# Hybrid decoder block on one core: the sums of the second MLP weight, on VectorE or by adding transfers

## The chip, the core and the metric

The kernel runs on one core of a Trainium2 chip. The core has five engines, each with a queue of its own that is worked off in order: PE (TensorE, matrix products), DVE (VectorE), ACT (ScalarE), POOL (GpSimd) and SP (SyncE, which here only issues transfers). SP, ACT and POOL can all issue transfers; these run on the same sixteen DMA engines. Queues wait for each other by semaphores.

The metric is the time of one execution in microseconds (us), the median of several runs.

## What is computed

One layer of a decoder: a mixer of two parts (gated linear attention and an S5 state-space layer), its output projection, and an MLP with a squared ReLU, over 512 tokens (and 16 meta tokens) of width 1024, in float32. The change lies in the MLP:

```python
hn = rmsnorm(h, g_ffn_pre[l])
f = jnp.square(jax.nn.relu(hn @ w_ff1[l])) @ w_ff2[l]
h = h + rmsnorm(f, g_ffn_post[l])
```

`w_ff1` is 1024 x 4096 and `w_ff2` 4096 x 1024. Below, f stands for the squared ReLU, kept in SBUF with its 4096 features on the partitions (32 blocks of 128) and the 512 tokens beside.

## The kernel before

**Products in three passes.** Each float32 operand is split into a rounded part ("hi", made by ScalarE, L152) and the rest ("lo", made by VectorE: L165 for weights of the first product, L1305 for those of the second). TensorE then makes three matmuls, hi x hi, hi x lo and lo x hi. A weight tile of 512 KB comes in on SyncE's queue as `wraw` (three buffers), is split into `whi` and `wlo` (three buffers each), and feeds the matmuls.

**The first MLP product.** For each of the 32 blocks of features (m), a tile of w1 is loaded (L158) and split, and 24 matmuls give the block; `relu2` (L1265) puts ReLU on ScalarE and the square on VectorE into f. The first three blocks run early, before all of hn is there. hh and hl are the two parts of hn, transposed.

**The second MLP product, by seven products.** f and w2 are taken as 2 x 2 blocks: tokens in two halves of 256, feature blocks even and odd, output columns in two halves of 512. `quarters` gives a11, a12 (first half of the tokens, even and odd blocks) and a21, a22 (second half); `b_of(k, n)` gives the blocks of w2, b11 to b22. Seven products of such blocks, with sums of blocks as operands, take the place of eight. Sums of f: s1 = a21 + a22, s2 = s1 - a11, s3 = a11 - a21, s4 = a12 - s2, made by VectorE in SBUF. Sums of w2: T1 = b12 - b11, T2 = b22 - T1, T3 = b22 - b12, T4 = b21 - T2.

**The sums of w2.** `weight_sums(j)` (L1254) does this for one pair of blocks j of 16: POOL loads 1 MB of w2 (`w2raw`, L1257), VectorE makes four sums of 128 x 512 (`w2t`, L1259 to L1262), POOL writes them, 1 MB, to DRAM (`t2d`, L1263). It is called after every second block of the first product, and twice behind it. There are two buffers of each kind.

**How the seven products run.** `product` (L1330) takes eight tiles; for each it calls `operands`, which loads 512 KB of w2 or of a sum from DRAM (L1302) and splits both sides, and then `step` twice, 12 matmuls in all. The order of the seven is a11 b11, s1 T1, s2 T2, a12 b21, s3 T3, s4 b22, a22 T4. X, Y and Z are the pairs of PSUM banks in which they are gathered. At the start of the products ScalarE's queue issues five loads of 512 KB (L1290, L1294): the gain `gff` and h of the four token tiles, which are wanted only at the end, when the second RMSNorm and the residual are done.

**What sets the order.** The code is written per tile; a scheduler puts it into the queues, and brings work forward where its operands and buffers allow. TensorE is held to the written order where `pinned` is set, which is so in the seven products and not from the first product's fourth block to its end. SBUF that one pool gives back is used by the next: the tiles of the pool `pout` (gff, h, c and others, from L1288) lie where hh, hl and the buffers of the sums were, so writing them waits until those are read.

## Time and profile before

| | |
|---|---|
| median of 3 runs | 907.79 us (906.01 to 909.96) |
| the profiled execution, its own time | 905.13 us |
| its span, first to last instruction | 903.4 us |
| mean granted TensorE clock | 0.997 |
| first MLP product from its fourth block | 583.0 to 743.1 us |
| the seven products | 743.1 to about 893 us |
| the end behind them (norm, residual, stores) | to 903.4 us |

A row of a group reads: line, engine, operation, output<-input by the program's names, shapes, how many; then busy time in us and the mean of one in ns; then the time that the engine stood idle just before them, and what ended it. A row of waits reads: who waited <- for whom: us in total, how often, the longest. A row of stretches gives the length, for each engine its busy time and how many instructions, the granted clock, the mean busy share of the sixteen DMA engines, and GB/s. A DMA row gives the issuing queue, how many, KB each, and the median us from issue to landing. Times in a timeline are us from the span's start.

A matmul of 512 columns reads 0.39 us, but matmuls overlap; what counts is the distance of their starts.

### The profile page before, as it was taken

The page shows a single profiled execution, that of the slowest core. Times are in us where ns is not written, and L with a number is a line of the kernel's source. Part 1 is how long each engine was busy: PE and PEld are TensorE (multiplying, and loading weights), DVE is VectorE, ACT ScalarE, POOL GpSimd, SP SyncE. Part 2 cuts the span into 40 slices and gives each one's busy share as a digit, 9 for nine tenths or more (in the row PEclk, how much of TensorE's full clock was granted, in tenths as well). Part 3 has the DMA queues.
Part 4 walks back from the last instruction along what each step waited for, and adds up shares of the span by engine and source line. Part 5 has one row for each costly group of instructions (what it writes and reads, how often), then busy time and mean ns, then how long its engine had stood idle before and what let it go on. Part 6 is the DMA issues. An engine that isn't in the chain of part 4 may idle for free.

```text
span 903.4 us, 13494 instructions
## 1 busy us (share of the span) xinstructions
PE 889.7 (98%) x4994; PEld 759.5 (84%) x4994; DVE 669.9 (74%) x1204; ACT 407.5 (45%) x667; POOL 88.4 (10%) x166
## 2 busy tenths in 40 slices
PE   8999999999999999999999999999999999999996
PEld 6899899898988888888888888988877888888885
DVE  7779998887877699876344765767866448778786
ACT  6362355466563444225222544422322326665763
POOL 1311100010101201103000000111220000000001
PEclk9999999999999999999999999999999999999998
DMA  7824644444435546468645772599999337656564
GB/s 211 218 96 131 192 113 111 104 120 112 105 110 134 161 106 178 125 188 267 184 144 147 214 209 70 188 364 369 391 397 320 112 105 269 209 188 201 171 210 139
DMA packets 171955, 166.68 MB, mean 185 GB/s; under 512 B 22397, under 2 KB 137153, under 8 KB 171890
## 3 DMA queue, kind: packets, MB, share of 16 engines
q1 hardware_dynamic: 155920, 110.48, 43.1%
q0 software_dynamic: 14768, 51.34, 15.1%
q10 hardware_dynamic: 1202, 4.00, 1.4%
q8 instruction: 39, 0.64, 0.3%
q14 instruction: 26, 0.21, 0.1%
HBM read 131.42 MB, written 34.37 MB: 184 GB/s over the span
## 4 chain that ended last, share of the span: by engine, by line
PE 83%; DMA 8%; DVE 4%; issue 3%; ACT 1%; POOL 1%; DVEq 0%; POOLq 0%
PE mm L60 58%; PE sm L60 22%; DMA w2raw<-in_w_ff_dram 8%; PE sm L65 3%; DVE wlo L165 1%; DVE w2t L1262 0%; DVE w2t L1260 0%; DVE w2t L1259 0%; POOL t2d L1263 0%; DVE xn L314 0%; DVE w2t L1261 0%; DVE xl L195 0%; DVE c L1368 0%; PE mm L65 0%; DVE f L1268 0%
## 5 line engine op out<-in xcount | busy, mean ns | idle before, releaser
L152 ACT ACTIVATE whi<-wraw 128x1024 fp32r<-128x1024 f32 x160 | 168.5, 1055 | 234.9 <-PE mm L60 182.7
L60 PE MATMUL mm<-xh,whi 128*128 128x512 f32 (+2 forms) x544 | 182.8, 336 | 0.3 <-ACT xh L152 0.3
L60 PE MATMUL mm<-xh,wlo 128*128 128x512 f32 (+2 forms) x544 | 178.9, 329 | 0.2 <-DVE wlo L165 0.2
L60 PE MATMUL mm<-xl,whi 128*128 128x512 f32 (+2 forms) x544 | 178.6, 328 | 0.3 <-DVE xl L195 0.3
L165 DVE TENSOR_TENSOR wlo<-wraw,whi 128x1024 fp32r<-128x1024 f32 x104 | 126.9, 1221 | 55.0 <-ACT whi L152 50.1
L60 PEld LDWEIGHTS mm<-xh,whi 128*128 128x128 f32 x544 | 102.8, 189 | 10.9 <-issue 1.2
L60 PEld LDWEIGHTS mm<-xh,wlo 128*128 128x128 f32 x544 | 102.7, 189 | 9.5 <-DVE wlo L165 0.4
L60 PEld LDWEIGHTS mm<-xl,whi 128*128 128x128 f32 x544 | 102.9, 189 | 8.9 <-DVE xl L195 0.5
L60 PE MATMUL mm<-hh,wlo 128*128 128x512 f32 (+1 forms) x280 | 104.1, 372 | 1.7 <-DVE wlo L165 1.7
L60 PE MATMUL mm<-hh,whi 128*128 128x512 f32 (+1 forms) x280 | 104.0, 371 | 0.0
L60 PE MATMUL mm<-hl,whi 128*128 128x512 f32 (+1 forms) x280 | 103.8, 371 | 0.0
L1305 DVE TENSOR_TENSOR wlo<-wraw,whi 128x1024 fp32r<-128x1024 f32 x56 | 68.4, 1223 | 23.4 <-ACT whi L152 23.4
L60 PE MATMUL sm<-wlo,fh 128*128 128x512 f32 x192 | 74.8, 390 | 0.0
L60 PE MATMUL sm<-whi,fl 128*128 128x512 f32 x192 | 74.7, 389 | 0.0
L60 PE MATMUL sm<-whi,fh 128*128 128x512 f32 x192 | 74.7, 389 | 0.0
L60 PEld LDWEIGHTS mm<-hh,wlo 128*128 128x128 f32 x280 | 52.7, 188 | 11.6 <-DVE wlo L165 2.5
L60 PEld LDWEIGHTS mm<-hh,whi 128*128 128x128 f32 x280 | 52.7, 188 | 9.1
L60 PEld LDWEIGHTS mm<-hl,whi 128*128 128x128 f32 x280 | 52.7, 188 | 8.9
L152 ACT ACTIVATE fh<-f 128x512 fp32r<-128x512 f32 x48 | 30.2, 630 | 49.9 <-PE sm L60 27.1
L60 PE MATMUL mm<-gh,whi 128*128 128x512 f32 x128 | 49.8, 389 | 0.0
L60 PE MATMUL mm<-gl,whi 128*128 128x512 f32 x128 | 49.8, 389 | 0.0
L60 PE MATMUL mm<-gh,wlo 128*128 128x512 f32 x128 | 49.8, 389 | 0.0
(413 smaller groups left out, 1575.5 us busy)
## 6 DMA issues: line engine op xcount, KB each, us to landing
wraw<-in_w_ff_dram SPq DMA_DIRECT2D x56, 512.0 KB, 4.8
wraw<-in_w_in_dram SPq DMA_DIRECT2D x48, 512.0 KB, 4.3
w2raw<-in_w_ff_dram POOLq DMA_DIRECT2D x16, 1024.0 KB, 9.3
t2d<-w2t POOLq DMA_DIRECT2D x16, 1024.0 KB, 7.1
wraw<-t2d SPq DMA_DIRECT2D x32, 512.0 KB, 3.8
wraw<-in_w_glu_dram SPq DMA_DIRECT2D x16, 512.0 KB, 3.9
M<-kpad SPq DMA_DIRECT2D x64, 64.0 KB, 2.5
wraw<-in_w_o_gla_dram SPq DMA_DIRECT2D x8, 512.0 KB, 4.5
```

The costliest lines, as they stand in the source:

```text
L60: ins = nc.tensor.matmul(*args, **kw)
L65: ins = nc.tensor.transpose(*args, **kw)
L152: S.activation(dst, src, AF.Copy, scale=scale)
L165: V.tensor_sub(lo, raw, f32(hi))
L1305: V.tensor_sub(bl, raw, f32(bh))
```

## The change

The signs of the seven products are turned so that every sum of w2 is made by additions alone: s1 = a21 - a22, s2 = s1 - a11, s3 = a11 - a21, s4 = a12 + s2, and T1 = b11 + b12, T2 = T1 + b22, T3 = b12 + b22, T4 = T2 + b21. Where a result has the wrong sign, it is subtracted at the end instead of added. The sums of w2 are no longer made by VectorE but by transfers that add to what stands at their destination in SBUF (`accum_op=ALU.add`), all issued by POOL.

T2 and T4 are made in eight chains of six transfers of 512 KB: load b11, add b12, add b22, write T2 to DRAM, add b21, write T4 to DRAM. Four chains run interleaved (buffers `acc`), then four more. Two transfers are issued behind each block of the first product from the fourth on: ScalarE copies one element of the block's ReLU into `flags`, POOL copies it into `seen`, and the transfers stand behind that copy on POOL's queue.

T1 and T3 are made as they are used: `fetch_sum` loads b11 or b22 on SyncE's queue into a buffer `added` (five of them), POOL adds b12 to it, and `operands` splits that buffer. It is called four tiles ahead of use; for the first four tiles this is in the last four tiles of the product before. DRAM holds two sums instead of four.

```diff
-    td2 = mk(dr, [4, NJ, P, 512], tag="t2d")
+    td2 = mk(dr, [2, NJ, P, 512], tag="t2d")
...
-        V.tensor_add(s1[:, 2 * jj : 2 * jj + 2], a21, a22)
+        V.tensor_sub(s1[:, 2 * jj : 2 * jj + 2], a21, a22)
         V.tensor_sub(a21, a11, a21)
...
-    def weight_sums(j):
-
-        raw = mk(pw2, [P, 2, D], tag="w2raw", bufs=2)
-        nc.gpsimd.dma_start(raw, w2[2 * j * P : (2 * j + 2) * P, :].rearrange("(k p) n -> p k n", p=P))
-        t_ = mk(pw2, [P, 4, 512], tag="w2t", bufs=2)
-        V.tensor_sub(t_[:, 0], raw[:, 0, 512:], raw[:, 0, :512])
-        V.tensor_sub(t_[:, 1], raw[:, 1, 512:], t_[:, 0])
-        V.tensor_sub(t_[:, 2], raw[:, 1, 512:], raw[:, 0, 512:])
-        V.tensor_sub(t_[:, 3], raw[:, 1, :512], t_[:, 1])
-        nc.gpsimd.dma_start(td2[:, j].rearrange("i p n -> p i n"), t_)
+    def weight_sums(jj):
+
+        acc = mk(pw2, [P, 2, 512], tag="acc", bufs=4)
+        nc.gpsimd.dma_start(acc, b_of(0, 0)(jj))
+        yield
+        nc.gpsimd.dma_start(acc, b_of(0, 1)(jj), accum_op=ALU.add)
+        yield
+        nc.gpsimd.dma_start(acc, b_of(1, 1)(jj), accum_op=ALU.add)
+        yield
+        nc.gpsimd.dma_start(t_of(0)(jj), acc)
+        yield
+        nc.gpsimd.dma_start(acc, b_of(1, 0)(jj), accum_op=ALU.add)
+        yield
+        nc.gpsimd.dma_start(t_of(1)(jj), acc)
+        yield
...
     def relu2(m, ps):
         r_ = mk(pff, [P, SEQ], tag="relu", bufs=2)
         S.activation(r_, ps, AF.Relu)
         V.tensor_mul(f[:, m], r_, r_)
+        S.copy(flags[:, m : m + 1], r_[:1, :1])
+        return G.tensor_copy(seen[:, m : m + 1], flags[:, m : m + 1])
...
+    todo = [interleaved([weight_sums(g + i) for i in range(4)]) for g in range(0, NJ // 2, 4)]
+    todo = (step for chain in todo for step in chain)
     for m in range(EARLY, MF):
         ps = bank("mm")
         feat_tile(load_w(w1[:, m * P : (m + 1) * P])[0], hh, hl, 0, SEQ, ps)
-        relu2(m, ps)
+        there = relu2(m, ps)
         if m % 4 == 3:
             early_sums(m // 4)
-        if m % 2 == 0:
-            weight_sums(m // 2 - 2)
-    for j in (NJ - 2, NJ - 1):
-        weight_sums(j)
+
+        with tc.issue_after(there.ins):
+            for _ in range(2):
+                next(todo, None)
...
+    def fetch_sum(b, jj):
+
+        raw = added[b, jj] = mk(po_, [P, 2, 512], tag="added", bufs=5)
+        nc.sync.dma_start(raw, b_of(0, 0)(jj) if b == "T1" else b_of(1, 1)(jj))
+        nc.gpsimd.dma_start(raw, b_of(0, 1)(jj), accum_op=ALU.add)
+
     def operands(a, b, jj):
-        raw = mk(wp, [P, 2, 512], tag="wraw", bufs=3)
-        nc.sync.dma_start(raw, b)
+        if (b, jj) in added:
+            raw = added.pop((b, jj))
+        else:
+            raw = mk(wp, [P, 2, 512], tag="wraw", bufs=3)
+            nc.sync.dma_start(raw, b(jj))
...
+    LEAD_SUMS = 4
...
+            if following and jj >= n - LEAD_SUMS:
+                fetch_sum(following, jj - n + LEAD_SUMS)
+            if isinstance(b, str) and jj + LEAD_SUMS < n:
+                fetch_sum(b, jj + LEAD_SUMS)
...
-        V.tensor_sub(a12, a12, a11)
+        V.tensor_add(a12, a12, a11)
...
-    product(X, a_of(0), b_of(0, 0), True)
+    product(X, a_of(0), b_of(0, 0), True, following="T1")
     take([c[:, left] for c in cs_[:2]], X)
-    product(Y, s1_of, t_of(1), True, to_s2)
+    product(Y, s1_of, "T1", True, to_s2)
     take(p5, Y)
-    product(X, a_of(0), t_of(2), False)
+    product(X, a_of(0), t_of(0), False)
     take([c[:, right] for c in cs_[:2]], X)
-    product(Z, a_of(1), b_of(1, 0), True, closes=True)
+    product(Z, a_of(1), b_of(1, 0), True, closes=True, following="T3")
...
-    product(X, a_of(2), t_of(3), False, to_s4)
+    product(X, a_of(2), "T3", False, to_s4)
     take([c[:, right] for c in cs_[2:]], X)
     for t in range(2):
-        V.tensor_add(cs_[2 + t][:, right], cs_[2 + t][:, right], p5[t])
+        V.tensor_sub(cs_[2 + t][:, right], p5[t], cs_[2 + t][:, right])
...
-        V.tensor_add(cs_[t][:, right], cs_[t][:, right], Y[t])
+        V.tensor_sub(cs_[t][:, right], Y[t], cs_[t][:, right])
```

How the queues stand, at three places. First SyncE's queue at the start of the seven products, with the semaphores that each row waits for (DVE: a buffer was split; PE: matmuls have read; DMAHW and DMASW: transfers have landed). Before, from the first product's fifth tile (`wraw_7397`, counted as tile 4 from 0) to the second product's first two tiles, which are T1 from DRAM:

```order
L1302 DMA wraw_7397<-in_w_ff_dram 128x2x512 [waits DMAHW2_49,DVE_49]
L1302 DMA wraw_7419<-in_w_ff_dram 128x2x512 [waits DMAHW3_49,DVE_49]
L1302 DMA wraw_7441<-in_w_ff_dram 128x2x512 [waits DMAHW4_49,DVE_49]
L1302 DMA wraw_7463<-in_w_ff_dram 128x2x512 [waits DMAHW5_49,DVE_49]
L1302 DMA wraw_7487<-t2d_6063 128x2x512 [waits DMAHW6_49,DMASW4_49,DMAHW7_49,DMASW2_49,DVE_49]
L1302 DMA wraw_7510<-t2d_6063 128x2x512 [waits DMASW6_49,DMAHW4_49,DMASW0_49,DVE_49]
```

After, from the same fifth tile (now `wraw_7394`) to the third product's first tile (`wraw_7675`, T2 from DRAM); `wraw_7419`, `wraw_7444` and `wraw_7469` are tiles 5, 6 and 7 of the first product:

```order
L1344 DMA wraw_7394<-in_w_ff_dram 128x2x512 [waits DMAHW2_49,DVE_49]
L1336 DMA added_7391<-in_w_ff_dram 128x2x512 [waits DMASW5_49,DMASW4_49,DMASW6_49,DMASW0_49,PE_49]
L1336 DMA added_7416<-in_w_ff_dram 128x2x512
L1344 DMA wraw_7419<-in_w_ff_dram 128x2x512 [waits DMAHW3_49,DVE_49]
L1336 DMA added_7441<-in_w_ff_dram 128x2x512 [waits DMAHW4_49]
L1336 DMA added_7466<-in_w_ff_dram 128x2x512 [waits DMAHW6_49]
L1336 DMA added_7493<-in_w_ff_dram 128x2x512 [waits DMAHW0_49,DMASW7_49]
L1344 DMA wraw_7444<-in_w_ff_dram 128x2x512 [waits DMAHW1_49,DVE_49]
L1344 DMA wraw_7469<-in_w_ff_dram 128x2x512 [waits DMAHW5_49,DMAHW2_49,DVE_49]
L1344 DMA wraw_7675<-t2d_6063 128x2x512 [waits DMAHW3_49,DMASW4_49,DVE_49]
```

Two loads of T1 stand before the first product's tile 5 and three more before tile 6; the first of them waits for TensorE to have made the first MLP product's last matmul.

Second VectorE's queue in the first MLP product. Before:

```order
L1259 TENSOR_TENSOR w2t_6758<-w2raw_6756 128x512
L1261 TENSOR_TENSOR w2t_6758<-w2raw_6756 128x512
L1260 TENSOR_TENSOR w2t_6758<-w2raw_6756,w2t_6758 128x512
L1262 TENSOR_TENSOR w2t_6758<-w2raw_6756,w2t_6758 128x512
L165 TENSOR_TENSOR wlo_6538<-wraw_6535,whi_6537 128x1024
L1268 TENSOR_TENSOR f_6061<-relu_6445 128x512
```

After:

```order
L165 TENSOR_TENSOR wlo_6512<-wraw_6509,whi_6511 128x1024
L1294 TENSOR_TENSOR f_6061<-relu_6423 128x512
L165 TENSOR_TENSOR wlo_6550<-wraw_6547,whi_6549 128x1024
L1294 TENSOR_TENSOR f_6061<-relu_6461 128x512
L1350 TENSOR_TENSOR fl_7354<-f_6061,fh_7353 128x512
```

The four sums that stood ahead of a split and waited for w2raw are gone.

Third POOL's queue at the end of the chains. Before, it goes from load to write and back, up to the last block:

```order
L1257 DMA w2raw_7218<-in_w_ff_dram 128x2x1024
L1263 DMA t2d_6063<-w2t_7144 128x4x512
L1257 DMA w2raw_7262<-in_w_ff_dram 128x2x1024
L1263 DMA t2d_6063<-w2t_7220 128x4x512
L1257 DMA w2raw_7270<-in_w_ff_dram 128x2x1024
```

After, with the waits:

```order
L1277 DMA t2d_6063<-acc_6660 128x2x512 [waits DMASW0_49]
L1277 DMA t2d_6063<-acc_6662 128x2x512 [waits DMASW1_49]
L1296 COPY seen_6068<-flags_6067 1x1 [waits Activation_49]
L1277 DMA t2d_6063<-acc_6700 128x2x512 [waits DMASW2_49]
L1277 DMA t2d_6063<-acc_6702 128x2x512 [waits DMASW3_49]
L1296 COPY seen_6068<-flags_6067 1x1 [waits Activation_49] x5
L1337 DMA added_7391<-in_w_ff_dram 128x2x512 [waits DMAHW6_49,DVE_49,PE_49]
```

The chains' last transfers stand five blocks before the end of the first MLP product (the five copies behind them), and the adding transfers of T1 come next, each behind its load.

28 lines of the change are left out of this document (20 added, 8 removed).

## The prediction

> **What bounds the kernel now.** I read the page first, then the stretches of the second half, then who waits for whom there, then the DMA's landing times at the start of the seven products. The page:
>
> ```profile
> span 903.4 us, 13494 instructions
> ...
> PE 889.7 (98%) x4994; PEld 759.5 (84%) x4994; DVE 669.9 (74%) x1204; ACT 407.5 (45%) x667; POOL 88.4 (10%) x166
> ...
> w2raw<-in_w_ff_dram POOLq DMA_DIRECT2D x16, 1024.0 KB, 9.3
> t2d<-w2t POOLq DMA_DIRECT2D x16, 1024.0 KB, 7.1
> ```
>
> TensorE is busy all but 14 us, so the change can take away little and can add only by making TensorE wait. The stretches: the first MLP product with the weight sums beside it (583 to 690), its rest (690 to 743), the seven products (743 to 895):
>
> ```profile
> core 0: us, PE busy (x) PEld busy (x) DVE busy (x) ACT busy (x) POOL busy (x), PEclk, DMA share, GB/s
> 583.00:670.00 87.00, 87.00 (x386) 72.05 (x385) 66.02 (x94) 26.39 (x35) 18.73 (x26) 1.00 1.03 373
> 670.00:690.00 20.00, 18.34 (x80) 14.54 (x79) 13.00 (x19) 6.16 (x8) 2.60 (x4) 1.00 1.02 373
> 690.00:743.00 53.00, 53.00 (x235) 43.89 (x234) 24.02 (x29) 13.90 (x18) 0.76 (x1) 1.00 0.47 139
> 743.00:895.00 152.00, 152.00 (x671) 125.51 (x670) 122.13 (x159) 94.93 (x133) 2.16 (x4) 1.00 0.62 201
> ```
>
> The clock is full throughout (1.00). While the sums are made the DMA engines are full (share above 1, 373 GB/s), and TensorE loses 1.7 us once, at 670 to 690. The seven products lose nothing. The waits between 583 and 743 say what the 1.7 us is:
>
> ```profile
> ACT whi L152 <- DMA wraw<-in_w_ff_dram: 36.0, 8, 6.1
> DVE w2t L1259 <- DMA w2raw<-in_w_ff_dram: 26.0, 14, 4.1
> ...
> PE mm L60 <- DVE wlo L165: 1.7, 2, 1.1
> ```
>
> ScalarE waited for w1's tiles, which shared the full DMA with the sums' transfers; TensorE felt two of those waits. Now the start of the products, where I expect the change to bite. First two rows of TensorE's timeline, the first matmul and one 60 matmuls later:
>
> ```profile
> 743.07 0.39 PE L60 MATMUL sm<-whi,fh 128*128 128x512 f32 x1
> ...
> 756.67 0.39 PE L60 MATMUL sm<-whi,fh 128*128 128x512 f32 x1
> ```
>
> The transfers issued from 742 to 746 (KB each, median us to landing):
>
> ```profile
> h<-hd ACTq DMA_DIRECT2D x4, 512.0 KB, 7.8
> gff<-in_g_ffn_post_dram ACTq DMA_DIRECT2D x1, 512.0 KB, 4.3
> wraw<-in_w_ff_dram SPq DMA_DIRECT2D x1, 512.0 KB, 8.1
> ```
>
> What the DMA moved from 746 to 754, and then, for comparison, the plain tile loads issued after 765:
>
> ```profile
> DMA packets 1060, 3.08 MB, mean 385 GB/s; under 512 B 95, under 2 KB 95, under 8 KB 1060
> ```
>
> ```profile
> wraw<-t2d SPq DMA_DIRECT2D x28, 512.0 KB, 3.8
> wraw<-in_w_ff_dram SPq DMA_DIRECT2D x16, 512.0 KB, 3.5
> ```
>
> And the product's sixth tile in the timeline, its issue and its split on ScalarE and VectorE:
>
> ```profile
> 745.39 3.55 SPq L1302 DMA_DIRECT2D wraw<-in_w_ff_dram  x2
> ...
> 753.58 1.06 ACT L152 ACTIVATE whi<-wraw 128x1024 fp32r<-128x1024 f32 x1 [3.29 <-DMA wraw<-in_w_ff_dram]
> ...
> 754.67 1.23 DVE L1305 TENSOR_TENSOR wlo<-wraw,whi 128x1024 fp32r<-128x1024 f32 x1 [3.05 <-ACT whi L152]
> ```
>
> 60 matmuls in 13.60 us make 0.227 us each, so a tile of a product (12 matmuls) is 2.72 us, a w1 tile (24) 5.44. Call 743.07 t0; tile k (from 0) starts at t0 + 2.72k. Tile 5 was issued at 745.39, landed 8.1 us later at 753.5 instead of in 3.5 because gff and the four h loads ran beside it, and was split by 755.90, 2.4 us after landing. Its matmuls began at 756.67: 0.8 us to spare. This place has no slack for more traffic, though the stretch as a whole moves only 201 GB/s.
>
> **The change, part by part.** *Sums on VectorE, removed.* Rows of the tile w2t:
>
> ```profile
> L1262 DVE TENSOR_TENSOR w2t<-w2raw,w2t x16: 682/685/694, 583.1 to 690.7; 128x512 f32<-128x512 f32 x16
> L1263 POOL DMA_DIRECT2D t2d<-w2t x16: 762/777/784, 584.1 to 691.6; - x16
> L1259 DVE TENSOR_TENSOR w2t<-w2raw x15: 686/692/694, 583.7 to 685.9; 128x512 f32<-128x512 f32 x15
> ```
>
> 64 additions of 0.69 us are 44 us of VectorE, and its 26 us of waiting for w2raw goes too. VectorE was busy 79 of the 107 us to 690 and TensorE ran beside it, so this is worth nothing by itself. What it frees is the 1.7 us above, and only if w1's loads then land in time.
>
> *Chains to DRAM.* 48 transfers of 512 KB, two behind each w1 tile for 24 of 29 tiles, half of them adding. How much of the DMA an adding transfer takes, no row shows. The nearest are the plain ones: below, the same 512 KB once (price p = 1); above, the destination fetched as well, like a second transfer of equal size (p = 2). I take p = 1.5, since neither end is nearer. Per w1 tile the DMA then moves w1's 0.524 MB, a plain 0.524 and an adding 0.524p: 289 GB/s over 5.44 us at p = 1, 337 at 1.5, 385 at 2. At 1.5 that is under the 373 to 385 of the rows, so w1's tiles come in time: -1.7 us. What is late next is nothing; TensorE is full. At p = 2 the gain is gone. POOL issues 64 transfers at 0.78 us instead of 32, 50 us in 310, with nobody near behind it. The chains end five w1 tiles (27 us) before t0; that covers the gff and h loads, which wait on ScalarE's queue for the chains' last transfers. If the cover goes, ScalarE stands still with the first product's splits behind it (rival B).
>
> *Flags.* 32 copies of one element on ScalarE and 32 on POOL. Nearest rows on ScalarE, a one-column read-out and a 512-column copy:
>
> ```profile
> L844 ACT ACTIVATION_READ_ACCUMULATOR osq<-sm 128x1 f32 x16 | 3.1, 194 | 0.0
> ...
> L1345 ACT COPY c<-sm 128x512 f32<-128x512 f32 x6 | 3.5, 577 | 0.0
> ```
>
> At 0.19 (the row of like size) that is 6 us, at 0.58 18 us, in a stage where ScalarE idles 75 of 107 us: nothing. Signs: an addition becomes a subtraction of the same form: nothing.
>
> *Sums made as the products are fed: the term that decides.* By the order of SyncE's queue in the changed program, the loads of the first product's tiles 5 and 6 have five new loads ahead of them: two of T1 before tile 5, three more before tile 6. They can't start early: the first waits for TensorE's last matmul on hh and hl, so all begins at t0, just when gff and h are loaded too. Five tiles of 0.524 MB (gff, h) on ScalarE's queue, five of T1 and two of the product on SyncE's are 6.29 MB. POOL's adding transfers start as each T1 load lands and share the engines; I count three of the five before tile 6 has landed, 1.57p MB. At 385 GB/s, plus 2.1 us that a lone load takes beyond its bytes (3.5 - 0.524/0.385), tile 6 lands at
>
> (6.29 + 2.36)/0.385 + 2.1 = t0 + 24.6 us for p = 1.5.
>
> Its matmuls are due at t0 + 16.3 and the split needs 2.4 us, so it was wanted at t0 + 13.9: TensorE waits **10.7 us** in all before tile 6 (part of it already at tile 5, which is not added again). At p = 1 it is 8.6, at p = 2 12.7; if the adding transfers gave way entirely, 4.5. Tile 7 follows one transfer later, 1.4 us, inside a tile's 2.72.
>
> [...]
>
> The later sums: buffers of T1 and T3 come round five tiles later, 13.6 us, less 2.4 for the split: 11.2. A load of 3.5, an issue of 0.8 and an adding transfer of 3.5 to 4.9 fit; nothing, and up to 3 us if p = 2 fills the DMA there (three units in 2.72 us ask for 578 GB/s). Five of T3's sums are fetched some 40 us ahead: nothing. The reads of T2 and T4 come as before.
>
> Sum: 10.7 - 1.7 = +9.0 us. The profiled execution took 905.13 (span 903.4 and 1.7 around it), which becomes 914.1. The median of the runs before is 907.79, 2.7 above it; I put the same 9.0 on it: **917 us**.
>
> **Rivals.** A, not slower: tiles 5 and 6 land in time after all. The point is 13.9 us for tile 6. Even with the adding transfers giving way, 6.29 MB in 11.8 us is 533 GB/s, which speaks against it; for it, the engines might serve SyncE's queue ahead of gff and h, which aren't wanted until the end: 3.67 MB then take 9.5 + 2.1 us, in time. But in the trace h's 7.8 us and the tile's 8.1 show both sharing. Time 907.8 - 1.7 = 906.1.
>
> B, adding transfers far dearer, p = 3: a w1 tile would then ask for 0.524 x 5 = 2.62 MB, 6.8 us at 385 GB/s instead of 5.44. Over 24 tiles that is 33 us too much; the five uncovered tiles take back 20 (27 less 1.4 for each tile's own load), 13 us stay, and 16.8 come at tile 6 by the formula above: 907.8 + 29.8 = 938. For it speaks that no row shows such a transfer; against it, that plain ones run at the full rate from POOL too.
>
> C, the five-tile round of the buffers doesn't hold: load, issue and addition take 3 us more than 11.2, once in T1 and once in T3, with tile 6 as forecast: 917 + 6 = 923.
>
> **How the numbers follow.** Forecast 0.65, A 0.15, B 0.12, C 0.08. The forecast's own range is 910.6 (4.5 - 1.7) to 923 (12.7 and 3, no gain). The range 905.5 to 926 takes in A and C and leaves out B and a little. A measurement here tells about 0.5% (4.5 us) from no change. Slower by more needs 912.3: C, B and most of the forecast, 0.76; within it A and the cheap end of the forecast, 0.22; faster, 0.02, out of A, since TensorE idles too little.
>
> **What would show it.** Tile loads of the first product landing some 15 us after issue; TensorE waiting at about t0 + 14 to t0 + 25 for wlo or whi, about 10 us and almost nowhere else; no wait for wlo at 670 to 690; VectorE some 44 us less busy; the DMA full for about 25 us from t0. Wrong would be: no wait of TensorE there; waits spread over each tile of T1 and T3; or a w1 stage longer than before.

## The result and the profile after

The changed kernel takes 934.25 us (median of 6 runs, 926.54 to 939.47), the kernel before, run beside it, 906.42: a ratio of 1.0296, 95% interval 1.0266 to 1.0326. A second set of six runs gave 935.16 us (928.41 to 940.71) and 1.0306 (1.0265 to 1.0347). So the change costs 28 us; 9 were forecast. The executions of the changed kernel lie further apart (13 us) than those of the kernel before (4 us), and the profiled one, 926.54 us, is the shortest of its six. Experiment 5 profiles another, of 931.80.

The lines of the page that answer to those shown of before:

```profile
span 924.8 us, 13502 instructions
...
PE 898.8 (97%) x4994; PEld 762.7 (82%) x4994; DVE 629.6 (68%) x1140; ACT 413.1 (45%) x699; POOL 144.8 (16%) x230
...
acc<-in_w_ff_dram POOLq DMA_DIRECT2D x32, 512.0 KB, 9.6
...
t2d<-acc POOLq DMA_DIRECT2D x16, 512.0 KB, 8.3
added<-in_w_ff_dram SPq DMA_DIRECT2D x16, 512.0 KB, 7.4
added<-in_w_ff_dram POOLq DMA_DIRECT2D x16, 512.0 KB, 9.9
```

VectorE is 40 us less busy (forecast 44), POOL 56 us more. TensorE's 898.8 busy us don't tell the loss: waits are not in them, and a matmul at half clock counts as busy (0.63 us in the timeline below, 0.40 at full clock). The stretches show both (granted clock third from the end, then the DMA share and GB/s). The first row is the first MLP product; the next three lie in the first of the seven products (741 to 776), the last two in T1's (776 to 804):

```profile
core 0: us, PE busy (x) PEld busy (x) DVE busy (x) ACT busy (x) POOL busy (x), PEclk, DMA share, GB/s
583.00:741.00 158.00, 158.00 (x699) 130.82 (x698) 66.65 (x79) 52.25 (x91) 58.90 (x77) 1.00 0.99 259
...
748.00:756.00 8.00, 7.27 (x29) 4.99 (x28) 3.56 (x4) 3.16 (x5) 2.46 (x2) 1.00 1.05 378
756.00:764.00 8.00, 5.13 (x12) 3.35 (x12) 2.43 (x3) 1.34 (x3) 1.20 (x1) 0.79 1.08 295
764.00:772.00 8.00, 3.49 (x8) 2.47 (x9) 3.03 (x4) 2.57 (x4) 2.39 (x2) 0.57 1.11 271
...
782.00:792.00 10.00, 7.77 (x35) 6.10 (x33) 2.69 (x4) 2.30 (x4) 3.57 (x4) 1.00 0.97 223
792.00:800.00 8.00, 7.09 (x17) 5.27 (x18) 5.10 (x6) 5.02 (x7) 1.75 (x2) 0.57 1.11 241
```

In these rows from 756 on the DMA engines are full (0.97 to 1.11) while they move only 223 to 295 GB/s; before, a share above 1 went with 373. In the first MLP product this execution lost nothing, and the 1.7 us of before are gone. Behind 741 TensorE waits where the forecast said, and in T1 too. Who it waits for from 741 on, and the transfers issued from 741 to 772 with their median us to landing:

```profile
PE sm L60 <- ACT whi L152: 8.4, 2, 5.7
PE sm L60 <- DVE wlo L1347: 3.7, 8, 0.8
PE sm L60 <- ACT fh L152: 1.3, 1, 1.3
```

```profile
added<-in_w_ff_dram SPq DMA_DIRECT2D x5, 512.0 KB, 16.3
added<-in_w_ff_dram POOLq DMA_DIRECT2D x5, 512.0 KB, 10.7
h<-hd ACTq DMA_DIRECT2D x4, 512.0 KB, 9.6
wraw<-in_w_ff_dram SPq DMA_DIRECT2D x3, 512.0 KB, 15.6
```

Tile 6 was issued at 751.24, landed at 766.85 and had its first matmul at 768.05, behind the 5.7 us. The adding transfers' price can be read from the queues between 772 and 820, since in that stretch POOL's queue (q0) carries adding transfers alone and the hardware queue (q1) plain ones (packets, MB, share of the sixteen engines):

```profile
q0 software_dynamic: 2459, 4.73, 54.2%
q1 hardware_dynamic: 4049, 7.81, 47.9%
```

The adding ones moved 4.73 MB in 54.2% of 48 us, 182 GB/s of the time that they took; the plain ones 7.81 MB in 47.9%, 340 GB/s. An adding transfer takes 1.9 times a plain one. The packets of both queues are of one size (4.73 MB in 2459 and 7.81 MB in 4049, 1.9 KB each), so smaller packets are not the reason.

The last new thing is the clock. TensorE's timeline in T1, behind the second long wait:

```profile
792.44 0.80 PE L60 MATMUL sm<-whi,fh 128*128 128x512 f32 x1 [2.67 <-ACT whi L152]
793.71 0.80 PE L60 MATMUL sm<-wlo,fh 128*128 128x512 f32 x1 [0.47 <-DVE wlo L1347]
794.30 0.63 PE L60 MATMUL sm<-whi,fl 128*128 128x512 f32 x1
794.73 0.63 PE L60 MATMUL sm<-whi,fh 128*128 128x512 f32 x1
...
799.31 0.40 PE L60 MATMUL sm<-whi,fl 128*128 128x512 f32 x1
799.54 0.40 PE L60 MATMUL sm<-whi,fh 128*128 128x512 f32 x1
```

Starts lie 0.43 us apart up to 799, then 0.23 again; the row of stretches gives 0.57 as the clock there, and the granted clock from 792.5 to 798.9 alone is 0.50.

### The profile page after: what moved, and what is told of

The parts are those of the page before. It is cut to its first block, busy times and chain, and to the rows that moved or that the text cites. A ratio compares the mean times of both kernels' runs of the same rounds, so it can differ in the third digit from the quotient of the medians.

```text
span 924.8 us, 13502 instructions
## 1 busy us (share of the span) xinstructions
PE 898.8 (97%) x4994; PEld 762.7 (82%) x4994; DVE 629.6 (68%) x1140; ACT 413.1 (45%) x699; POOL 144.8 (16%) x230
## 4 chain that ended last, share of the span: by engine, by line
PE 85%; DMA 8%; DVE 3%; ACT 1%; issue 1%; POOL 0%; DVEq 0%; ACTq 0%; POOLq 0%; SPq 0%
PE mm L60 69%; PE sm L60 13%; DMA added<-in_w_ff_dram 4%; PE sm L65 3%; DMA wraw<-in_w_ff_dram 3%; DVE wlo L1347 1%; DMA wraw<-t2d 1%; ACT whi L152 1%; DVE xn L314 0%; DVE c L1405 0%; DVE xl L195 0%; DVE fl L1350 0%; DMA grow<-in_g_mix_pre_dram 0%; DVE c L1411 0%; PE mm L65 0%
## 5 line engine op out<-in xcount | busy, mean ns | idle before, releaser
L152 ACT ACTIVATE whi<-wraw 128x1024 fp32r<-128x1024 f32 x144 | 151.8, 1057 | 258.4 <-PE mm L60 152.3
L165 DVE TENSOR_TENSOR wlo<-wraw,whi 128x1024 fp32r<-128x1024 f32 x104 | 127.0, 1222 | 122.8 <-ACT whi L152 118.0
L60 PEld LDWEIGHTS mm<-xh,whi 128*128 128x128 f32 x544 | 102.8, 189 | 10.9 <-issue 1.2
L60 PE MATMUL sm<-whi,fh 128*128 128x512 f32 x192 | 77.9, 406 | 9.6 <-ACT whi L152 8.4
L60 PE MATMUL sm<-wlo,fh 128*128 128x512 f32 x192 | 77.9, 406 | 3.7 <-DVE wlo L1347 3.7
L60 PE MATMUL sm<-whi,fl 128*128 128x512 f32 x192 | 77.2, 402 | 0.2
L1347 DVE TENSOR_TENSOR wlo<-wraw,whi 128x1024 fp32r<-128x1024 f32 x40 | 48.8, 1222 | 32.0 <-ACT whi L152 31.9
L60 PEld LDWEIGHTS sm<-whi,fh 128*128 128x128 f32 x192 | 37.5, 195 | 19.7 <-ACT whi L152 10.0
L60 PEld LDWEIGHTS sm<-wlo,fh 128*128 128x128 f32 x192 | 37.5, 195 | 15.0 <-DVE wlo L1347 7.1
```

The costliest lines, as they stand in the source:

```text
L60: ins = nc.tensor.matmul(*args, **kw)
L152: S.activation(dst, src, AF.Copy, scale=scale)
L165: V.tensor_sub(lo, raw, f32(hi))
L1347: V.tensor_sub(bl, raw, f32(bh))
```

## Experiments

Time lost by TensorE is compared from here on by one measure: from 583 us on, whatever two matmuls' starts lie apart beyond 0.227 us (0.05 and less is not counted), so waits and half clock together. By it the kernel without sums (experiment 7) loses 0.3 us, and the other profiles, by stage:

| kernel (profiled execution) | w1 stage | a11 b11 | T1 | T2 | later | sum |
|---|---|---|---|---|---|---|
| before (905.13) | 2.2 | 0 | 0 | 0 | 0.3 | 2.5 |
| changed (926.54) | 0 | 13.3 | 6.5 | 1.9 | 1.9 | 23.7 |
| changed, experiment 5 (931.80) | 5.0 | 15.2 | 3.5 | 4.7 | 0.8 | 29.2 |
| 1, all transfers plain (915.44) | 0 | 10.4 | 0.8 | 0 | 0.2 | 11.4 |
| 2, chains alone (911.25) | 4.8 | 0.1 | 0 | 0 | 0.2 | 5.2 |
| 3, h late (932.35) | 7.7 | 6.4 | 2.9 | 5.0 | 4.0 | 26.1 |
| 9, T1 and T3 late (940.09) | 5.2 | 0 | 13.9 | 0 | 14.2 | 33.3 |
| 10, the same, all plain (910.89) | 0 | 0 | 5.9 | 0 | 2.2 | 8.1 |
| 13, T1 late (930.25) | 5.4 | 0 | 15.0 | 4.8 | 1.8 | 26.9 |
| 14, feeds alone (929.89) | 0 | 14.0 | 4.4 | 6.8 | 2.1 | 27.2 |

"w1 stage" is the first MLP product from 583 us, "later" all behind T2. The sums for the two executions of the changed kernel, 23.7 and 29.2, differ by 5.5 us, their times by 5.3.

### 1. All transfers plain

```diff
-        nc.gpsimd.dma_start(acc, b_of(0, 1)(jj), accum_op=ALU.add)
+        nc.gpsimd.dma_start(acc, b_of(0, 1)(jj))
...
-        nc.gpsimd.dma_start(raw, b_of(0, 1)(jj), accum_op=ALU.add)
+        nc.gpsimd.dma_start(raw, b_of(0, 1)(jj))
```

(and likewise the two other additions of a chain)

> The changed kernel with each adding transfer made a plain one into the same buffer, in the same place of the same queue and of the same size (the sums are not made, so the output is another). Theory (an adding transfer takes about twice the DMA time of a plain one; this sets the load of the w1 stage and the late sums of T1): the DMA share between 583 and 741 falls from 0.99 to about 0.7 at about the same 259 GB/s; tile 6 of the first product lands some 2 us earlier but still late, as five T1 loads, gff and the h loads stay ahead of it, so that TensorE waits about 8.6 us in the first product; the T1 product waits under 1 us where the changed kernel lost about 7; some 2 to 3 us are lost to matmuls at half clock; no wait in the w1 stage. Time about 915 us (910 to 919), 2% under the changed kernel. Rival (the order of the queues alone decides, the price of an adding transfer does not matter): waits as in the changed kernel and 930 to 936 us. Rival (the adding price is all of it): no waits, about 904 us.

915.94 us, ratio 1.0080 (1.0051 to 1.0109). Its stretches:

```profile
583.00:741.00 158.00, 158.00 (x705) 131.12 (x704) 68.35 (x80) 52.59 (x92) 49.35 (x78) 1.00 0.78 260
741.00:820.00 79.00, 72.00 (x301) 57.38 (x300) 50.35 (x58) 41.74 (x57) 9.96 (x14) 0.96 0.88 311
```

The same GB/s as the changed kernel in the first MLP product, at a share of 0.78 in place of 0.99: 0.21 of 158 us over 24 adding transfers is 1.4 us for each beyond its plain price. T1 loses 0.8 us instead of 3.5 to 6.5. The price is worth 18 to 19 of the 28 us. What stays is the first product: the longest wait, for tile 6, is 5.6 us even with plain transfers, as five loads of T1, gff and h are ahead. That tile landed 22.3 us behind the product's first matmul; the prediction's formula gives 22.5 for p = 1. TensorE's waits from 741 on:

```profile
PE sm L60 <- ACT whi L152: 5.6, 1, 5.6
```

### 2. The chains alone

```diff
-    product(Y, s1_of, "T1", True, to_s2)
+    product(Y, s1_of, t_of(0), True, to_s2)
...
-    product(X, a_of(2), "T3", False, to_s4)
+    product(X, a_of(2), t_of(1), False, to_s4)
```

(and no `following`)

> The changed kernel with its paced chains, but without the sums that are added as their products are fed: those two products read the stored sums of the chains instead (so two of the seven products have other data, and the output is another). Theory: the loss lies in the fed sums alone, and the chains gain what was forecast, the waits of the w1 stage: about 904 us (902 to 906), no wait of TensorE on whi over 1 us behind 741. Rival (the chains themselves hold up the end of the w1 stage or leave the DMA engines busy beyond it, so that the first tiles of the products are late): 908 us or more, with waits in the first product.

909.10 us, ratio 1.0014 (0.9996 to 1.0033): the chains gain nothing. The theory's 904 missed. TensorE's waits from 680 to 745:

```profile
PE mm L60 <- DVE wlo L165: 1.6, 3, 0.5
PE mm L60 <- ACT whi L152: 1.6, 3, 0.9
```

Three tiles of w1 came late, at 701, 708 and 737. The first of the seven products lost 0.1 us, so the chains reach no further than the w1 stage.

### 3. gff and h late

```diff
-    nc.scalar.dma_start(gff, io["g_ffn_post"][0].partition_broadcast(P))
...
-        nc.scalar.dma_start(ht, h_dram[t])
...
-    take([c[:, right] for c in cs_[:2]], X)
+    taken = take([c[:, right] for c in cs_[:2]], X)
+    with tc.issue_after(taken.ins):
+        nc.scalar.dma_start(gff, io["g_ffn_post"][0].partition_broadcast(P))
+        for t in range(TT):
+            nc.scalar.dma_start(hts[t], h_dram[t])
```

> The changed kernel with gff and the four loads of h (2.62 MB) issued on ScalarE's queue only behind the copies that close the third product, about 55 us later. Theory (tile 6 of the first product waits for all bytes issued ahead of it, and gff and h are a third of them): 2.62 MB at 385 GB/s are 6.8 us, so TensorE's wait for tile 6 falls from 5.7 us to under 1, and the half clock behind it goes with it (about 2 us more); the second half of the T1 product still loses 3 to 7 us, since the adding transfers alone set its pace. About 8 to 9 us under the changed kernel, 925 us (921 to 929). Rival (gff and h run beside on other engines' time, the order of SyncE's queue alone decides): no change beyond 2 us, 932 to 935 us. Rival (the late sums of T1 are late because of h, too): no wait in T1 either, below 919 us.

929.83 us, ratio 1.0229 (1.0188 to 1.0269), some 5 us under the changed kernel where 8 to 9 were expected. SyncE's queue also came out in another order (fewer T1 loads ahead of tile 6). The first product lost 6.4 us instead of 13 to 15, now at tile 7; but behind the third product, where the 2.62 MB now ran, 4.0 us were lost instead of 1 to 2. Behind 741 it lost 18.4 us in place of 24 in all; the 7.7 us of the w1 stage, which the edit does not touch, are a tile of w1 that came 3.8 us late. So gff and h or the order beside them are a part of the wait, smaller than the theory had, and some of the loss moved along with their bytes. How much of it is gff and h alone is not shown, as both changed.

### 4. The kernel before, only paced

```diff
-            weight_sums(m // 2 - 2)
+            with tc.issue_after(there.ins):
+                weight_sums(m // 2 - 2)
```

(an edit of the kernel before, with `flags` and `seen` as in the change)

> The kernel before, its sums on VectorE and its signs as they were, with only the pacing of the change: a flag is written by ScalarE and read by POOL behind each tile of the w1 stage, and the loads and stores of the sums are issued behind it. Theory (the gain forecast for the w1 stage comes from the pacing, since the sums' loads no longer come in bursts ahead of the tiles of w1): TensorE's waits of 1.7 to 2.4 us there vanish and nothing else changes: 904 us, 0.2 to 0.3% under the kernel before. Rival (the waits come from VectorE's sums, which delay wlo; they go only with the sums): the waits stay, 906 to 907 us.

959.11 us, ratio 1.0562 (1.0539 to 1.0585): far off either theory. The waits from 583 to 775 say why:

```profile
DVE w2t L1259 <- DMA w2raw<-in_w_ff_dram: 76.3, 12, 9.2
PEld mm L60 <- DVE wlo L165: 21.1, 9, 4.0
PE mm L60 <- DVE wlo L165: 17.3, 9, 3.6
```

The loads went out later, but VectorE's additions stood where they had stood; VectorE waited for them 76 us instead of 26, with the wlo of the next tile of w1 behind it in the queue. The edit said nothing about pacing as such. Experiment 12 repeats it with the additions moved too.

### 5. The changed kernel again

> The changed kernel once more, for a second profile of it: the first profile is of its shortest execution (926.5 us beside a median of 934), in which TensorE lost nothing between 583 and 741. Theory (the DMA engines are full in the w1 stage, so that in most executions a tile of w1 also comes late there): a median of 933 to 935 us; in the profile a wait of TensorE of 2 to 4 us on a tile of w1 somewhere between 650 and 741, with a stretch of half clock behind it, some 6 us in all; the waits at tile 6 of the first product and in the second half of T1 as in the first profile, together about 17 us with the half clock behind them. Rival (the w1 stage never waits, the same waits in the products are only longer): no wait over 0.5 us ahead of the first product.

935.16 us (928.41 to 940.71). TensorE's waits from 575 to 745, in the w1 stage:

```profile
PEld mm L60 <- ACT whi L152: 2.9, 1, 2.9
...
PE mm L60 <- ACT whi L152: 2.5, 1, 2.5
```

One tile of w1 came 2.5 us late at 700, with half clock behind it, 5.0 us in all, as expected. In the first product tile 6 was issued at 754.61 and landed at 773.49, 28.0 us behind that product's first matmul (745.5); TensorE waited 11.7 us for it. T1 lost 3.5 us and T2 4.7: together, from the first product on, the same 24 us as in the first profile (17 were expected), otherwise shared out.

### 6. Waits filled with matmuls

```diff
+            for i in range((fill or {}).get(jj, 0)):
+                PE.matmul(idle, before[0][:, i % 2, :P], before[2][:, i % 2, :], start=True, stop=True)
             for t in range(2):
                 step(acc, t, ops, first and jj == 0, jj == NJ // 2 - 1)
+            before = ops
```

(`fill` is {5: 7, 6: 24} in the first product and {6: 12} in T1's; `idle` is an unused bank)

> The changed kernel with 43 more matmuls on operands that are there already, into a bank that is not used: 7 ahead of tile 5 and 24 ahead of tile 6 of the first product, 12 ahead of tile 6 of the T1 product, where TensorE waited 1.4, 5.7 and 2.8 us. They make up 1.6, 5.4 and 2.7 us at 0.227 us each, so they fill the waits and add next to nothing where the wait is as long. Theory (half clock follows from the idle stretch and costs its own time): no matmuls at half clock in these two products, about 5.5 us under the changed kernel (2.9 in the first product, 2.8 in T1), 928 to 930 us. Rival (the transfers set the pace anyway, and the slow matmuls only take up time in which the next tile would be waited for): the same time within 1.5 us, with longer waits at the tiles behind.

934.18 us, ratio 1.0290 (1.0255 to 1.0326), against 935.16 and 1.0306 for the changed kernel on the same chip: the same, as the rival said. But the run is a weak test. The extra matmuls are 9.8 us; from the first product on TensorE lost 12.7 us more, 22.5 in all, against 24. In the first product the fill did take up most of the wait, and tile 6 still began 27.0 us behind the first matmul (27.3 and 29.1 in the two profiles without fill): there the transfers set the pace. Half clock behind tile 6 stayed, for 3.4 us. In T1 the wait, 2.6 us, is ahead of tile 5, and the twelve extra matmuls stand ahead of tile 6, so they could not fill it. What half clock costs by itself this run does not show.

### 7. No sums

```diff
-        with tc.issue_after(there.ins):
-            for _ in range(2):
-                next(todo, None)
...
-    product(Y, s1_of, "T1", True, to_s2)
+    product(Y, s1_of, b_of(0, 1), True, to_s2)
```

(and plain quarters in place of T2, T3 and T4)

> The changed kernel with no sums of the second weight at all: no chains, no adding transfers, and in place of the four sums the products read plain quarters of the weight (four of the seven products have other data, the output is another). It is the bound for any way of making the sums. Theory (the chains cost nothing but DMA time, of which the w1 stage has too little): 903 to 904 us, no wait of TensorE over 0.3 us behind 583, and DMA busy under 0.5 in the w1 stage; the chains alone, which took 909, then cost 5 us by late tiles of w1, in place of the 1.7 us that they were to gain. Rival (the chains cost nothing, and the time of the other runs is the scatter of executions): 907 to 909 us here too.

903.24 us, ratio 0.9950 (0.9929 to 0.9970). Its stretches:

```profile
583.00:741.00 158.00, 158.00 (x699) 130.85 (x699) 66.86 (x79) 52.54 (x91) 15.39 (x29) 1.00 0.34 100
741.00:820.00 79.00, 79.00 (x350) 65.46 (x349) 63.04 (x72) 49.40 (x66) 0.53 (x1) 1.00 0.67 219
```

This is the floor: with the rest of the kernel as it is, no way of making the sums can gain more than 4 us on the kernel before. Flags and turned signs are in this kernel and cost nothing. Against experiment 1, 0.44 of 158 us for the 48 plain transfers of the chains is 1.45 us each.

### 8. Waits of known length

```diff
+    waits = {5: 8, 9: 9, 13: 10, 17: 11, 21: 12, 25: 14, 29: 17}
...
+        if m - 2 in waits:
+            PE.matmul(ps[:, :P], tok[:, :P], tok[:, P : 2 * P], start=True, stop=True)
...
+        if m in waits:
+            with tc.issue_after(there.ins):
+                for _ in range(waits[m]):
+                    G.memset(tok, 1.0)
```

> The kernel without sums (experiment 7), with seven waits of TensorE made by work of POOL: behind the tiles 5, 9, 13, 17, 21, 25 and 29 of the w1 stage POOL fills a buffer 8, 9, 10, 11, 12, 14 and 17 times (0.54 us each), and a matmul of 128 columns two tiles later waits for it. The waits should come out at about 0.5, 1, 1.5, 2, 2.5, 4 and 5.5 us. Theory (half clock follows an idle stretch of 2 to 3 us or more): the first three leave the next matmuls at 0.227 us, those from about 2.5 us on are followed by some 13 matmuls at 0.427, 2.6 us more each; about 903 + 17 + 3 times 2.6 = 928 us. [...] Rival (half clock has another cause, as the load on the DMA engines): none at all, 920 us.

938.42 us in one run. The waits came out longer than planned: 1.5, 2.1, 2.6, 3.2, 3.8, 5.0 and 6.7 us, 24.9 in all. The stretches behind the last five, those that hold the last two waits themselves, and the one that holds the second:

```profile
616.00:631.00 15.00, 13.10 (x59) 10.61 (x58) 6.31 (x8) 5.20 (x9) 6.04 (x12) 1.00 0.34 100
...
655.00:663.00 8.00, 7.97 (x29) 6.44 (x30) 0.28 (x1) 0.56 (x1) 0.32 (x1) 0.79 0.22 66
...
682.00:690.00 8.00, 7.99 (x29) 6.46 (x30) 0.00 (x0) 0.58 (x1) 0.08 (x1) 0.79 0.22 66
...
710.00:718.00 8.00, 8.00 (x30) 6.40 (x29) 0.00 (x0) 1.04 (x2) 0.00 (x0) 0.79 0.19 56
...
724.00:739.00 15.00, 10.19 (x45) 8.24 (x44) 4.97 (x6) 3.63 (x7) 8.40 (x17) 0.97 0.36 105
739.00:747.00 8.00, 8.00 (x32) 6.47 (x31) 0.41 (x1) 1.50 (x2) 0.00 (x0) 0.85 0.01 2
754.00:769.00 15.00, 8.45 (x38) 6.74 (x37) 3.65 (x4) 3.47 (x6) 9.44 (x19) 0.88 0.33 105
769.00:777.00 8.00, 8.00 (x31) 6.48 (x31) 0.00 (x0) 1.01 (x2) 0.00 (x0) 0.80 0.00 0
```

A mean clock of 0.79 over 8 us is half clock for 0.21 x 8 x 2 = 3.4 us. The waits of 1.5 and 2.1 us are followed by none (matmuls behind them start 0.227 us apart), that of 2.6 and all longer ones by half clock, and it comes in one piece of 3.4 us, or two where the wait is 6.7 (3.3 us of it while still waiting). One piece costs 1.7 us of matmuls, not the 2.6 expected. The DMA's share is 0.00 to 0.36 in these rows, so its load is not the cause.

### 9. T1's and T3's loads behind the last tile

```diff
-            if following and jj >= n - LEAD_SUMS:
-                fetch_sum(following, jj - n + LEAD_SUMS)
...
+            if following and jj == n - 1:
+                with tc.issue_after(loads[-1].ins):
+                    for later in range(LEAD_SUMS):
+                        fetch_sum(following, later)
```

(`loads` holds the products' plain loads; a fifth fetch comes from T1 itself)

> The changed kernel with the first five loads for T1 (and for T3) issued on SyncE's queue behind the load of the last tile of the product before, in place of between its tiles 4 and 7; the adding transfers follow their loads. Theory (order puts the first product's wait there, but the adding transfers' rate is short of what T1 needs in any order): no wait over 0.5 us in the first product; T1's first sum lands about 20 us behind the first matmul of the seven products, as it is wanted, and the others 4.0 us apart where 2.7 are wanted, so that TensorE waits some 9 to 10 us over the T1 product, in steps of 1 to 2 us, and with little half clock; with the 4 to 5 us that the chains cost in the w1 stage and 2 in T3 some 920 to 925 us. Rival (the bytes are the same, the wait only moves from the first product to T1): 932 to 936 us. Rival (the order alone was wrong): 907 to 910 us, no wait in T1.

935.48 us, ratio 1.0313 (1.0293 to 1.0333): no gain. The first product lost nothing; T1 lost 13.9 us and T3 13.5. TensorE's waits behind 750:

```profile
PE sm L60 <- ACT whi L152: 13.6, 4, 4.4
PE sm L60 <- DVE wlo L1347: 4.5, 7, 0.8
```

The edit moved T3's loads too, which the theory had not counted, so this run could not say what the order is worth. Experiment 13 does.

### 10. The same with plain transfers

The edits of 9 and 1 together.

> The kernel of experiment 9 with each adding transfer made a plain one (the sums are not made, the output is another). Theory (order and price together are all of the loss): neither the w1 stage nor the products wait by more than 1 us in all, 903 to 906 us, under the kernel before. Rival (five loads in a burst behind tile 7 are late for T1 even as plain ones, as gff and h are under way): waits of 3 us or more at the start of T1, 908 us or more.

912.30 us, ratio 1.0069 (1.0053 to 1.0085), 3.6 us under experiment 1 and 6 above the theory's range. The first product lost nothing, T1 5.9 and T3 2.0 us: the rival. T1's sums take two transfers each, one behind the other, and five in a burst behind tile 7 beside gff and h come late even when plain.

### 11. The price in bursts

```diff
+        if m in (6, 12, 18, 24):
+            with tc.issue_after(there.ins):
+                for i, acc in enumerate(accs):
+                    if m in (6, 18):
+                        nc.gpsimd.dma_start(acc, b_of(0, 0)(i))
+                    else:
+                        nc.gpsimd.dma_start(acc, b_of(0, 1)(i), accum_op=ALU.add)
```

> The kernel without sums (experiment 7) with four bursts of eight transfers of 0.52 MB on POOL's queue in the w1 stage, into eight buffers that nothing reads: plain ones behind tile 6, adding ones into the same buffers behind tile 12, and both again behind tiles 18 and 24. Beside them only the loads of w1 run, 0.52 MB in 5.45 us or 96 GB/s. Theory (an adding transfer takes 1.9 times the DMA time of a plain one): with 385 GB/s for both, a plain burst takes 4.19 MB / 289 GB/s = 14.5 us from the first issue to the last landing, an adding one about 27 us. Rival (1.5 times, as the prediction took): about 22 us. Rival (the adding ones are late for another reason, the wait for the load that they add to or the issue on POOL of 1.2 us each, and not for their own time): about 15 to 17 us.

From the first issue to the last landing the plain bursts took 16.3 and 17.2 us, the adding ones 29.7 and 30.8. The queues from 607 to 624 (plain):

```profile
q0 software_dynamic: 1152, 4.19, 62.1%
```

and from 650 to 662 (adding):

```profile
q0 software_dynamic: 1045, 2.01, 90.2%
```

Plain: 4.19 MB in 62.1% of 17 us, 397 GB/s. Adding: 2.01 MB in 90.2% of 12 us, 186 GB/s. An adding transfer takes 2.1 times a plain one, 3.1 us between landings. Loads of w1 issued in an adding burst took up to 19 us to land (the two from 650 to 662 a median of 17.4), in a plain one up to 14 (the four from 607 to 624 a median of 7.7), instead of 4 (4.1 in the kernel before, from 690 to 735); the three buffers covered that here (902.84 us in one run).

### 12. The sums of before, spread

```diff
+    due = {}
+    for j in range(NJ):
+        due.setdefault(EARLY + max(0, (5 * j) // 3 - 1), []).append(j)
...
-        if m % 2 == 0:
-            weight_sums(m // 2 - 2)
+        with tc.issue_after(there.ins):
+            for j in due.get(m, ()):
+                w2_load(j)
+        with tc.issue_after(squared.ins):
+            for j in due.get(m - 2, ()):
+                w2_sums(j)
```

(`w2_load` and `w2_sums` are the two halves of before's `weight_sums`, `squared` the square of block m on VectorE)

> The kernel before with its sums on VectorE spread over the w1 stage: the 16 loads of the second weight go out by the flags of the change, behind the tiles 3, 3, 5, 7, 8 and so on to 27 in place of as early as buffers allow, and VectorE makes the sums of a load two tiles (11 us) later, behind the square of that tile. Same arithmetic as before. Theory (before, VectorE waits 26 us in that stage for loads in a burst that fills the DMA engines, with the wlo of a tile behind it; spread, the loads run at about 350 GB/s and are there when VectorE comes): no wait of TensorE in the w1 stage, 903.5 to 905 us, under both kernels. Rival (the sums cost TensorE time by VectorE's load in itself): 907 us. Rival (as in experiment 4, VectorE stands before loads that are late, now that they are paced): over 915 us.

903.49 us (12 runs, 902.20 to 907.02), ratio 0.9973 (0.9959 to 0.9986): faster than both kernels, than the one before by 0.3%, and within 0.3 us of the floor of experiment 7. The profiled execution is the longest, 907.02; what it has over the median lies ahead of 583. Its stretches:

```profile
583.00:670.00 87.00, 87.00 (x402) 72.79 (x402) 59.40 (x81) 31.10 (x55) 22.54 (x34) 1.00 0.87 302
670.00:690.00 20.00, 20.00 (x90) 16.56 (x89) 15.24 (x22) 5.80 (x11) 5.28 (x9) 1.00 0.88 302
690.00:745.00 55.00, 55.00 (x244) 45.59 (x243) 33.88 (x45) 17.35 (x30) 12.17 (x20) 1.00 0.91 316
```

Where the kernel before had the DMA full at 1.03 up to 690 and at 0.47 behind it, this one has it at 0.87 to 0.91 throughout, and TensorE loses 0.2 us from 583 on. The 1.7 us came from the burst of loads, not from VectorE's additions as such.

### 13. T1's loads alone late

Experiment 9 with T3's loads back in their place.

> Experiment 9 with the loads for T3 back at their place in the changed kernel; only the first five loads for T1 stand behind the last tile of the first product. In experiment 9 the T3 product alone waited some 10 us, which the changed kernel does not. Theory (adding transfers land 3.1 us apart at best, and 4 to 4.5 with plain ones between them, where T1 wants one in 2.7; so the order only chooses whether the first product or T1 waits, and saves what the first product's wait costs beyond that): no wait in the first product, about 10 us and 4 us of half clock in T1 as in experiment 9, 2 us in T3; 924 to 928 us, some 9 under the changed kernel. Rival (the loss is fixed by the bytes, whatever the order): 933 to 936 us.

930.31 us, ratio 1.0249 (1.0195 to 1.0304). The first product lost 0, T1 15.0, T2 4.8 us, together 19.8, where the changed kernel lost 21.7 and 23.4 in the three. The time lies between the theory's 924 to 928 and the rival's 933 to 936. The order chooses the place of the wait and is worth at most 2 to 5 us of the 28; the interval overlaps that of the changed kernel.

### 14. The feeds alone

The chains of experiment 7 taken out, T1 and T3 added as they are fed, plain quarters for T2 and T4.

> The changed kernel without the chains: T1 and T3 are added as they are fed, and in place of T2 and T4 the products read plain quarters of the second weight (two of the seven products have other data, the output is another). With experiment 2 (chains alone, 909), experiment 7 (neither, 903) and the changed kernel (both, 935) it splits the loss. Theory (the two parts add up: the chains cost 4 to 6 us by late tiles at the end of the w1 stage, the feeds the rest by waits in the first product, T1 and T3): 928 to 931 us, no wait in the w1 stage. Rival (the chains' adding transfers reach beyond the w1 stage and make the first product late): 920 us or less, with a wait for tile 6 under 3 us. Rival (the feeds alone are all of it): 934 to 936 us.

926.52 us, ratio 1.0220 (1.0179 to 1.0261), 1.5 us under the theory's range, and no loss in the w1 stage. With neither part 903.24, with the chains alone 909.10, with the feeds alone 926.52: added up, 932.4, against 934.25 and 935.16 with both. The parts add up within 3 us: 6 for the chains, 23 for the feeds.

## Why the prediction was wrong

Slower was right, and so were the mechanism and the place of its main term. The size was not: 917 us with 926 at the top, and 934 measured. By the measure of the experiments' table, less what the kernel before loses, the two profiles of the changed kernel give -2.2 and +2.8 us for the w1 stage (forecast -1.7), +13.3 and +15.2 for the first product (+10.7), and +10.0 and +8.7 for all behind it (nothing, up to 3). By its own steps:

*Sums on VectorE removed, -1.7 us.* Right in the first profile only. In the first MLP product a tile's transfers were to ask for 337 GB/s "at 1.5", under the row of 373. At the 2.1 of experiment 11 a tile moves 0.524 + 0.524 + 1.10 = 2.15 MB, which at 385 GB/s takes 5.58 us where TensorE needs 5.44. The DMA was full (0.99), and in five of the seven profiles with adding chains tiles of w1 came late: 5.0 us in the second profile, 5.9 us for the chains by experiments 2 and 7. The text had said that at p = 2 the gain is gone; it is a loss there. A longer w1 stage, one of its own signs of being wrong, came in the second profile.

*The price of an adding transfer, p = 1.5.* This step failed, and with it the later sums, below. The text bounded it by 1 and 2 and took the middle "since neither end is nearer"; no run shows 1.5. It is 1.9 to 2.1 (the changed kernel's queues, experiment 1, experiment 11), at or beyond the upper end. That the destination is fetched as well, the text's ground for that end, no run shows; the times alone were measured. The price alone does not make the 28 us: with 2.1 in the text's own terms (13.1 at tile 6, no gain in the w1 stage, 3 for the later sums) the sum is 16, or 924 us.

*The wait for tile 6, 10.7 us.* Mechanism and place were right: tile 5 landed 12 us and tile 6 15.6 us after issue. With 2.1 the prediction's formula moves the landing from t0 + 24.6 to t0 + 27.0 and the wait to 13.1; measured were t0 + 26.1 and t0 + 28.0, and TensorE began the tile 10.9 and 12.8 us late. That the first lies so near the 10.7 is in part luck: the price was too low, which takes 2.4 us off the landing, and the split was counted in full, 2.4 us, where the first matmul began 1.2 us after the landing. The path differed too: the text has all loads under way at t0, but SyncE's queue stood behind landings and issued tile 6 only 10.5 and 9.1 us after the first matmul. As the DMA was full throughout (1.00 from 741 to 769), bytes over rate held all the same. The other 2.4 us of the first product's 13.3 and 15.2 were lost behind tile 6's first matmul, to a late wlo and half clock. With the T1 loads moved behind the first product's tiles its wait was gone (experiments 9 and 13), and with gff and h moved, and the order changed with them, it was half (experiment 3); so these transfers made it. But most of the loss came back as waits in T1, T2 or behind.

*The later sums, "nothing, and up to 3 us".* The second failure and, at 9 to 10 us, the larger one. It follows from the first only in part. The sum was made for a round of buffers that takes 11.2 us, as if a transfer had the DMA to itself. The rate decides: T1 asks for a plain and an adding transfer per tile, 3.1 times 0.524 MB, 4.2 us at 385 GB/s, where a tile lasts 2.72; even the text's own 1.5 makes it 3.4. In the first profile the sum for T1's tile 5 took 5.1 us for its load and 9.6 for the addition, where the text had 3.5 and 3.5 to 4.9. The text saw the rate ("578 GB/s") and still put 3 us on it. T3's first five sums, said to be fetched far ahead for nothing, are loaded from 782 to 800, while T1's last additions run (to 797), and so 13 adding transfers, not 8, fall into the stretch up to 820. Its DMA share there is 1.02 of 79 us, 81 us of work:

```profile
741.00:820.00 79.00, 66.67 (x254) 50.81 (x252) 40.92 (x48) 33.84 (x46) 16.22 (x14) 0.89 1.02 280
```

Without sums it is 0.67 (experiment 7). T1, T2 and later lost 10.3 and 9.0 us.

*Flags and signs, nothing.* Right (experiment 7).

*The rivals.* A (tile 6 in time) did not occur. B's price of 3 was too dear, but its mechanism, a tile of w1 that asks for more than the DMA gives, is what the w1 stage showed. C was the second half of the truth, at 9 to 10 us instead of 6 and in T1 and T2 rather than T1 and T3, and its chance of 0.08 was too small. The top of the forecast's range does take p = 2 in all three terms (12.7, 3 and no gain); the fault is that 3 us stood beside the 578 GB/s that the sums ask for there, and "no gain" beside a w1 stage that at p = 2 asks for all that the DMA gives (385 GB/s). Half clock was in no term.

## What to carry to other kernels

Give a transfer that adds to its destination twice the DMA time of a plain one (1.9 to 2.1 times here), and hold the sum for a stage against the DMA's rate (385 GB/s in the trace of before) before asking which wait is where: a stage that asked for more than the rate lost the difference here in three orders of the queues (the changed kernel, experiments 9 and 13). When the range is made, put an unknown price into each stage's bytes over rate, and not only into the one wait that seems to decide. Where work beside TensorE makes it wait now and then, spread its transfers over the stage, with the engine that consumes them moved by as much, before replacing it: that took the kernel before to its floor (experiment 12), while moving the loads alone made it 5.6% slower (experiment 4).

## What the hardware showed unexpectedly

TensorE's half clock behind a wait. Experiment 8 shows it after single waits of 2.6 us and longer and not after 2.1, in pieces of 3.4 us, each at a cost of 1.7 us if there is work. In its trace the pieces begin at 656.08, 683.39, 710.69, 738.00 and 765.31 us, each 27.31 us behind the last, eight times 3.413, although the waits end at other distances (655.03, 682.01, 709.57, 738.27 and 768.56). So in that trace the clock changes at marks 3.413 us apart, wherever the wait lies. In the trace of the changed kernel, up to its last matmul, the pieces begin at 758.2 (3.413 us long), 765.0 and 792.3 us (6.827 us each), 6.8 and 27.3 us apart.

Held against such marks, the profiles of the changed kernel and of experiments 1, 3, 4, 6, 8 to 10, 13 and 14 agree from 583 us on. Idle is here what two starts lie apart beyond 0.227 us (0.427 at half clock). A stretch between two marks at full clock in which TensorE was idle for 2.1 us or more was followed by half clock every time (36 stretches); one with 1.8 us or less never was (40 with more than 0.8). In the changed kernel, up to its last matmul, the three ahead of half clock held 2.3, 2.9 and 2.7 us idle, every other at full clock 1.2 or less. So short waits add up: at 756.88 in the changed kernel waits of 1.4 and 0.5 us, 0.2 us of matmul between them, fell into one stretch with 2.3 us idle in all (the clock of 0.79 over 756 to 764 in the rows above). And the wait of 2.1 us in experiment 8 lay across a mark, with 1.6 us idle in the longer part, and passed.

Why the clock does so, no run here shows. In the changed kernel the matmuls at half clock add up to some 4 us of delay in the first profile and 3 in the second from the first product on; how much of that the time would lose without half clock is open, as the transfers are late beside it.
